# The last taps of the second depthwise convolution ahead of the key and value blocks of an encoder layer

## The chip, the cores and the metric

The kernel runs on one core of a Trainium2 chip. The metric is device time in microseconds (us) of one execution. Several executions of the kernel before gave a median of 944.46 us (the lowest 943.23). One more execution was profiled: it took 943.95 us, of which the profile covers a span of 941.9 us, from the first to the last instruction. What the profile calls PE is TensorE's matmul, PEld its weight load, DVE is VectorE, ACT is ScalarE, POOL is GpSimd and SP is SyncE, which here issues all DMAs.

## The reference

One layer over two sequences (256 and 2048 tokens of width 1024, with 16 meta tokens ahead of each):

```
h = rmsnorm(z, norm_w)
proj = einsum('bld,de->ble', h, w_in)
q, k, v, g_att, c_val, c_glu, g_conv = split(proj)
q = rmsnorm(q per head); k = rmsnorm(k per head)
att = windowed_gqa(q, k, v, sink) * silu(g_att)
u = c_val * sigmoid(c_glu)
y = depthwise_conv(u, conv_w, width 31) + conv_b
cnv = silu(layernorm(y, ln_w, ln_b)) * silu(g_conv)
out = z + einsum('ble,ed->bld', concat[att, cnv], w_out)
```

The convolution has 512 channels; the LayerNorm is over these channels, for each token.

## The kernel before, in words

The tokens are 18 blocks of 128 (numbers 0 to 17) and 16 meta columns, in six groups of three blocks, and the groups are two chunks: chunk 0 holds groups 0 to 2, chunk 1 groups 3 to 5 (blocks 9 to 17). The combined projection has eleven units of 256 columns. For each chunk they run in the order `ORDER`: four convolution units (`U_C`, 0 to 3), two gates of the convolution (`U_GC`, 4 and 5), two gates of the attention (`U_GA`, 9 and 10), then keys and values (`U_KV`, 8), then two units of queries (`U_Q`, 6 and 7). Each float32 product is made of three passes over split operands (`PASSES`), so one 128 by 256 block of `proj_te` (L873 to L887) is 24 matmuls at L879, and `proj_et` (L856 to L871) is 24 matmuls of up to 400 columns at L863.

After the projections comes the attention of 18 blocks with the output projection (L609). Its first steps are woven into the query units by `spread` (L658): at its 4th query block `attention_open` (L255) issues the first attention loads, at the 7th `q_prep(0)` runs, from the 8th on slots of the attention are handed out, and at the 9th `mixing_open` (L280) takes the memory of the convolution.

A chunk's convolution is four strips of 31 taps, each tap one DVE instruction over 128 by 1167 elements (L946; the first tap is L937), which adds to the strip `y`. The strips of odd and of even units wait in two lists, `conv_q`.

**What sets the order.** The program is written out in the order in which Python hands instructions out, and a scheduler may then move an instruction within its engine's order, by its own estimate of when operands are ready; the engines run that fixed order. Python's order around the projections is set by a ledger. After each block a `tick(ns)` (L177) adds the block's estimated nanoseconds to `credit`; while the credit is positive it takes taps from `conv_q`, at 1.04 * 1167 + 135 = 1348.7 each, and what is left over is dropped. Other DVE work is charged with `owe` (800 for one key and value block). A gate's half is worth 3912, a key and value or a query block 2640. `later(k, f)` hands `f` out at the end of the k-th tick from here; `store` is a DMA from SP two ticks on.

**Keys and values.** `kv_block` (L1023): 24 matmuls into one of four PSUM banks (tags a and b, two each); ACT makes two squared sums (L985) and the copy `vs` (L1028), POOL the inverse root `rqk` (L148, L149), DVE the low part of `vs` (L1029) and the scaled keys `kn` (L1037); PE transposes `kn` (L1047, tag d), ACT and DVE make `ks` (L1049, L1050); SP stores `vd` and, twice, `kd`.

**LayerNorm.** `ln_block` (L211) works on one block of 128 tokens: four transposes on PE (`lnt`, L221, tag c), statistics on DVE (L224, L225), an inverse root and an offset on POOL (L148, L149, L227), the normalised `zn` on DVE (L234; three buffers), four transposes back (`lnu`, L240, tag d or, once the attention is open, a), four Silu on ACT (L243), and a store `cd` by SP (L246). The last gate unit of a chunk puts its LayerNorm blocks into `ln_q` (L1247): blocks 0 to 7 for chunk 0, 8 to 17 for chunk 1. `tick` hands out at most one of them, when `ready` (L1241) says so: the chunk's last tap has been handed out, this was first seen at tick `seen`, and `LN_WAIT[c]` more ticks have passed.

Ahead of the last two units of the second chunk stands a loop that empties the lists of taps (`keys[-2]` is the first unit of queries of chunk 1):

```
1194  if (c, u) == keys[-2] and g == CHUNKS[c][0]:
1195      while conv_q[0] or conv_q[1]:
1196          tick(3000)
```

In the ledger of the kernel before, chunk 1 comes to its first key and value block (block 9) with a credit of -992 and seven taps left, all of the last strip. The ticks of blocks 9 to 13 hand out 1, 1, 2, 1 and 2 of them. The tick of block 14 finds none left; with `LN_WAIT[1]` = 1 the tick of block 15 hands out the first LayerNorm block, and those of blocks 16 and 17 and of the first seven query blocks the other nine. The loop finds the lists empty and does nothing.

Of the kernel before, what the change touches and what calls it, by code (L numbers as in the profile page):

```python
# [45 lines left out]
CACHE = 2  # L46
WST = 9
W0 = 3
LN_WAIT = (9, 1)
LTAGS = "dbdbd" + "dcdcddddd"  # L50
LTAGS_N = len(LTAGS)
MAN1 = {mybir.EngineType.Pool}
# [33 lines left out]
CHUNKS = [[0, 1, 2], [3, 4, 5]]  # L86
# [3 lines left out]
U_KV = 8  # L90
# [9 lines left out]
def hymba_kernel(  # L100
# [61 lines left out]
    def later(k, f):  # L162
        due.setdefault(clock[0] + k, []).append(f)
# [13 lines left out]
    def tick(ns):  # L177
        credit[0] += LOAD * ns
        if ln_q and not flushing[0] and ln_q[0][0]():
            ln_q.pop(0)[1]()  # L180
            ln_at[0] = clock[0]
            credit[0] -= 800
        while credit[0] > 0 and (conv_q[0] or conv_q[1]):
            side[0] ^= 1
            q = conv_q[side[0]] or conv_q[1 - side[0]]
            cost, f = q.pop(0)
            credit[0] -= cost
            f()
        credit[0] = min(credit[0], 0.0)
        clock[0] += 1  # L190
        for f in due.pop(clock[0], []):
            f()
# [508 lines left out]
    if True:  # L701
# [31 lines left out]
        class Prep:  # L733
# [6 lines left out]
            def load(self, d2):  # L740
                n = self.n
                self.xt[d2] = sp.tile([P, 2, 400], F32, tag="xt", name=f"xt{self.g}_{d2}", bufs=XTB)
                nc.sync.dma_start(
                    self.xt[d2][:, :, :n],
                    zt[2 * d2 : 2 * d2 + 2, :, self.c0 : self.c0 + n].rearrange("d p n -> p d n"),
                )
# [147 lines left out]
        def u_tiles(c, j):  # L894
            us[c, j] = cp.tile([P, UWID], F32, tag="us", name=f"us{c}_{j}")
            if c == 0:
                nc.gpsimd.memset(us[c, j][:, 271:286], 0.0)
            else:
                nc.gpsimd.tensor_copy(us[c, j][:, 0:30], carry[:, j, :])
                nc.gpsimd.memset(us[c, j][:, 1182:1197], 0.0)  # L900

        def c_group(c, j, ws, g):
            n = GROUPS[g][1]
            pg = proj_et(ws, 0, g)
            sg = sp.tile([P, 400], F32, tag="sg", name=f"sg{c}_{j}_{g}")
            nc.scalar.activation(sg[:, :n], pg[:, :n], AF.Sigmoid)  # L906
            tick(24 * (n / 2.4 + 3))
            pv = proj_et(ws, 1, g)
            if g == 0:
                dst = [(us[c, j][:, 0:271], 1, 272), (us[c, j][:, 286:301], 1, 16), (us[c, j][:, 301:429], 272, 400)]  # L910
            elif c == 0:
                o = 301 + 384 * g - 256
                dst = [(us[c, j][:, o : o + n], 0, n)]
            else:
                o = 30 + 384 * (g - 3)
                dst = [(us[c, j][:, o : o + n], 0, n)]
            for ap, a, b in dst:
                nc.vector.tensor_tensor(ap, pv[:, a:b], sg[:, a:b], op=ALU.mult)
            owe(600)
            tick(24 * (n / 2.4 + 3))  # L920
# [45 lines left out]
        def g_group(ws, t0, g):  # L966
            o = NM if g == 0 else 0
            for hi in range(2):
                ps = proj_et(ws, hi, g, o)
                so = gp.tile([P, 384], F32, tag="go", name=f"go{t0}_{hi}_{g}")  # L970
                nc.scalar.activation(so, ps[:, :384], AF.Silu)  # L971
                store(gd[t0 + hi, :, 384 * g : 384 * g + 384], so)
                tick(24 * 163)
# [86 lines left out]
        def kv_group(ws, g):  # L1060
            if g == 0:
                kv_block(ws, 0, 0, NM, -1)
                tick(24 * 107)
            for b in range(3 * g, 3 * g + 3):
                kv_block(ws, g, blk_local(b)[1], P, b)
                tick(24 * 110)

        ORDER = U_C + U_GC + U_GA + [U_KV] + U_Q
        keys = [(c, u) for c in range(2) for u in ORDER]
# [82 lines left out]
        def at_item_start(i, c, u, g):  # L1152
            if (c, u, g) == (1, ORDER[0], CHUNKS[1][1]):
                nc.sync.dma_start(km.bitcast(F32), kmd)
                for r0 in range(0, P, NM):
                    nc.sync.dma_start(vm[r0 : r0 + NM].rearrange("p a e -> p (a e)").bitcast(F32), vmd)
            if i == 0:
                for q in range(4):
                    w01[1][1](q, nc.gpsimd if q % 2 else nc.vector)
                for k in (4, 5, 6):  # L1160
                    r[k]()
            if i == 1:
                later(1, preps[1].first)
                later(1, preps[1].alloc)
                later(1, lambda: preps[1].scale(0))
                for q in range(4):
                    if q < 3:
                        later(1, lambda q=q: preps[1].scale(q + 1))
                    later(1, lambda q=q: preps[1].split(q))
                for k in range(7, 10):  # L1170
                    later(1, lambda k=k: later(1, stats(k)))
                for q in range(4):
                    later(2, lambda q=q: preps[2].load(q))
            if i == I2:
                later(1, preps[2].first)
                later(1, preps[2].alloc)
                later(1, lambda: preps[2].scale(0))
                for q in range(4):
                    if q < 3:
                        later(1, lambda q=q: preps[2].scale(q + 1))  # L1180
                    later(1, lambda q=q: preps[2].split(q))
# [9 lines left out]
        split_at += [(1, u, CHUNKS[1][1]) for u in U_C[1:]]  # L1191

        for i, (c, u, g) in enumerate(items):
            if (c, u) == keys[-2] and g == CHUNKS[c][0]:
                while conv_q[0] or conv_q[1]:
                    tick(3000)
            if u in U_C and g == CHUNKS[c][0]:
                u_tiles(c, u)
            ws = wsplit[c, u]
            at_item_start(i, c, u, g)  # L1200
            for t, p, what in prep_at.get(i, []):
                if what == "load":
                    for q in range(4):
                        later(1, lambda p=p, q=q: p.load(q))
                else:
                    later(1, p.first)
                    for q in range(4):
                        later(1 + q // 2, lambda p=p, q=q: p.scale(q))
            if u in U_C:
                c_group(c, u, ws, g)  # L1210
            elif u in U_Q:
                q_group(ws, u - U_Q[0], g, spread if (c, u) in keys[-2:] else lambda b: None)
            elif u == U_KV:
                kv_group(ws, g)
            elif u in U_GC:
                g_group(ws, 4 + 2 * (u - U_GC[0]), g)
            else:
                g_group(ws, 2 * (u - U_GA[0]), g)
            for k in loads.get(i, []):
                load, split = weights(k)  # L1220
                load(nc.sync)
                room = max(1, when[first_at[keys[k]]] - when[i + 1])
                for q in range(4):
                    at = max(1, min(room, W0 + q * min(WST, max(1, (room - 2) // 4))))
                    later(at, lambda split=split, q=q: split(q, nc.vector))
            if (c, u, g) in split_at:
                presplit_wo(split_at.index((c, u, g)))
            if c == 0 and u in U_GA:
                for k3 in range(3):
                    k = 10 + 3 * (3 * (u - U_GA[0]) + g) + k3  # L1230
                    if k <= NB:
                        later(1 + k3, lambda k=k: later(1, stats(k)))
            if (c, u) == (0, ORDER[-1]):
                p = preps[g + 3]
                p.alloc()
                for q in range(4):
                    later(1 + q // 2, lambda p=p, q=q: p.split(q))
            if u in U_C and g == CHUNKS[c][2]:
                conv(c, u, 0)
            if i == last_at[c, u] and u == U_GC[-1]:  # L1240
                def ready(c=c):  # L1241
                    if left[c, 0]:
                        return False
                    seen.setdefault(c, clock[0])
                    return clock[0] >= seen[c] + LN_WAIT[c]

                for b in range(0, 8) if c == 0 else range(8, NB):  # L1247
                    ln_block(c, b, ready)
# [66 lines left out]
```

## Time and profile before

| | |
|---|---|
| median of the runs | 944.46 us |
| profiled execution | 943.95 us |
| its span | 941.9 us |
| PE busy | 935.6 us (99%) |
| PEld busy | 886.3 us (94%) |
| DVE busy | 744.4 us (79%) |
| ACT busy | 421.8 us (45%) |
| POOL busy | 293.3 us (31%) |
| DMA | 176.49 MB, 187 GB/s on the mean |

The share of busy time is a mean over stages. A matmul's record is longer than the time until the next one starts, since matmuls are pipelined, so a busy PE shows only waits that are longer than that overlap; PEld, whose records are shorter, shows more of them. "Idle before" names what ended an engine's idle time. A row of the windows gives, for a stretch of the span, the busy time of each engine with the count of its instructions in brackets.

### The profile page before, as it was taken

The page shows a single profiled execution, that of the slowest core. Times are in us where ns is not written, and L with a number is a line of the kernel's source. Part 1 is how long each engine was busy: PE and PEld are TensorE (multiplying, and loading weights), DVE is VectorE, ACT ScalarE, POOL GpSimd, SP SyncE. Part 2 cuts the span into 40 slices and gives each one's busy share as a digit, 9 for nine tenths or more (in the row PEclk, how much of TensorE's full clock was granted, in tenths as well). Part 3 has the DMA queues.
Part 4 walks back from the last instruction along what each step waited for, and adds up shares of the span by engine and source line. Part 5 has one row for each costly group of instructions (what it writes and reads, how often), then busy time and mean ns, then how long its engine had stood idle before and what let it go on. Part 6 is the DMA issues. An engine that isn't in the chain of part 4 may idle for free.

```text
span 941.9 us, 16665 instructions
## 1 busy us (share of the span) xinstructions
PE 935.6 (99%) x5794; PEld 886.3 (94%) x5794; DVE 744.4 (79%) x1263; ACT 421.8 (45%) x1160; POOL 293.3 (31%) x490
## 2 busy tenths in 40 slices
PE   9999999999999999999999999999999999999998
PEld 8999999999999999999999999988888888888887
DVE  5579999997977879999996655677777677767773
ACT  7432022253457751011111356666666666656661
POOL 4320000173558400000000553755433242333332
PEclk9999999999999999999999999999999999999999
DMA  8575345676656595233333697975666556655512
GB/s 306 170 253 217 134 176 176 217 269 251 182 185 189 182 312 182 90 113 134 140 128 123 159 327 225 395 240 159 200 188 172 151 165 196 188 159 148 163 62 68
DMA packets 146211, 176.49 MB, mean 187 GB/s; under 512 B 40816, under 2 KB 108736, under 8 KB 146000
## 3 DMA queue, kind: packets, MB, share of 16 engines
q1 hardware_dynamic: 146128, 175.43, 57.8%
q8 instruction: 46, 0.75, 0.3%
q14 instruction: 37, 0.30, 0.1%
HBM read 112.69 MB, written 62.70 MB: 186 GB/s over the span
## 4 chain that ended last, share of the span: by engine, by line
PE 94%; DMA 2%; DVE 1%; SPq 1%; issue 0%; ACT 0%; POOL 0%; DVEq 0%; ACTq 0%; POOLq 0%
PE pj L863 43%; PE y L609 21%; PE pj L879 13%; PE O L533 5%; PE S L383 4%; PE pT_c L499 2%; PE pT_m L499 2%; PE pT_x L499 1%; DMA cd<-zn 1%; DMA bias<-in_bias_c 1%; PE qT L383 1%; PE lnu L240 0%; DMA xn<-in_z 0%; PE lnt L221 0%; DVE xt L772 0%
## 5 line engine op out<-in xcount | busy, mean ns | idle before, releaser
L863 PE MATMUL pj<-xh,ws 128*128 128x384 f32 (+1 forms) x1536 | 395.9, 338 | 0.1
L946 DVE SCALAR_TENSOR_TENSOR y<-us,cw,y 128x1167 f32<-128x1167 f32 x240 | 329.0, 1427 | 0.4
L863 PEld LDWEIGHTS pj<-xh,ws 128*128 128x128 f32 x1536 | 280.0, 188 | 0.4 <-ACT xh L1111 0.4
L863 PE MATMUL pj<-xl,ws 128*128 128x384 f32 (+1 forms) x768 | 260.9, 340 | 0.1
L609 PE MATMUL y<-wo,rest 128*128 128x512 f32 (+1 forms) x672 | 172.7, 394 | 0.0
L879 PE MATMUL pj<-ws,xh 128*128 128x256 f32 (+1 forms) x880 | 164.2, 284 | 0.3 <-DVE kn L1037 0.3
L863 PEld LDWEIGHTS pj<-xl,ws 128*128 128x128 f32 x768 | 144.1, 188 | 0.5 <-DVE xl L801 0.4
L609 PEld LDWEIGHTS y<-wo,rest 128*128 128x128 f32 x672 | 117.5, 189 | 21.4 <-DVE rest L566 0.3
L879 PEld LDWEIGHTS pj<-ws,xh 128*128 128x128 f32 (+1 forms) x880 | 136.1, 187 | 1.1 <-issue 0.4
L879 PE MATMUL pj<-ws,xl 128*128 128x256 f32 (+1 forms) x440 | 124.3, 283 | 0.0
L441 DVE CUSTOM_DVE_ANT_0 sb<-S,bias,vec 128x304 f32<-128x304 f32 (+5 forms) x144 | 74.5, 517 | 33.8 <-PE S L383 31.5
L453 ACT ACTIVATE sb<-sb,nm 128x304 f32<-128x304 f32 (+5 forms) x144 | 77.8, 540 | 48.9 <-DVE nm L441 48.2
L971 ACT ACTIVATE go<-pj 128x384 f32<-128x384 f32 x48 | 23.5, 489 | 149.8 <-PE pj L863 142.3
L879 PEld LDWEIGHTS pj<-ws,xl 128*128 128x128 f32 (+1 forms) x440 | 82.2, 187 | 0.2
L479 POOL TENSOR_SCALAR sb<-sb,es 128x304 f32<-128x304 f32 (+5 forms) x144 | 73.1, 525 | 16.0 <-DVE es L466 13.1
L561 POOL TENSOR_TENSOR at<-at,ga 128x256 f32<-128x256 f32 x36 | 26.5, 737 | 164.0 <-DVE at L555 104.8
L148 POOL TENSOR_SCALAR ssk<-ssk 128x2 f32<-128x2 f32 x18 | 8.4, 465 | 210.0 <-ACT sqk L985 210.0
L383 PEld LDWEIGHTS S<-kw,q 128*128 128x128 f32 x288 | 53.2, 188 | 10.6
L383 PE MATMUL S<-kw,q 128*128 128x304 f32 (+5 forms) x288 | 62.8, 299 | 0.0
L148 POOL TENSOR_SCALAR ssq<-ssq 128x4 f32<-128x4 f32 (+2 forms) x55 | 23.5, 427 | 98.3 <-ACT xn L726 74.4
L906 ACT ACTIVATE sg<-pj 128x384 f32<-128x384 f32 (+1 forms) x24 | 11.8, 492 | 82.9 <-PE pj L863 82.0
L609 PE MATMUL y<-wo,mch 128*128 128x512 f32 x144 | 47.2, 409 | 0.0
(139 smaller groups left out, 1306.9 us busy)
## 6 DMA issues: line engine op xcount, KB each, us to landing
wd<-ws SPq DMA_DIRECT2D x36, 512.0 KB, 5.8
ws<-wd SPq DMA_DIRECT2D x36, 512.0 KB, 6.2
wraw<-in_w_in SPq DMA_DIRECT2D x52, 256.0 KB, 6.3
xn<-in_z SPq DMA_DIRECT2D x18, 512.0 KB, 5.5
gd<-go SPq DMA_DIRECT2D x48, 192.0 KB, 2.2
yo<-in_z SPq DMA_DIRECT2D x36, 256.0 KB, 3.9
out_y<-yo SPq DMA_DIRECT2D x35, 256.0 KB, 2.7
wo<-wod SPq DMA_DIRECT2D x16, 512.0 KB, 7.4
```

The costliest lines, as they stand in the source:

```text
L148: nc.gpsimd.tensor_scalar(src, src, scale, eps, op0=ALU.mult, op1=ALU.add)
L383: r = f(*a, **k)
L441: nc.vector.tensor_tensor_reduce(out=sb[:, n, c0:c1], in0=ps[:, 0:w], in1=cst["bias"][:, kv, at + c0 : at + c1], scale=1.0, scalar=nsnk[:, ...
L453: nc.scalar.activation(sb[:, n, c0:c1], sb[:, n, c0:c1], AF.Exp, bias=nm[:, n : n + 1], scale=-1.0, accum_out=rs[:, n : n + 1],)
L479: nc.gpsimd.tensor_scalar(sb[:, k, a0:a1], sb[:, k, a0:a1], es[:, k : k + 1], 1.0, op0=ALU.mult, op1=ALU.mult)
L499: nc.tensor.transpose(pt[: c1 - c0, n, :], sbt[b, kv][:, n, c0:c1], ident)
L533: nc.tensor.matmul(opj[b, kv][:, n0:n1], t[:r, kv, :], p[:r, n0:n1], start=(k == "c" and i == 0), stop=(k == "x" and i == len(work) - 1),)
L561: nc.gpsimd.tensor_tensor(at[:, pr, :], at[:, pr, :], gat[b][:, pr, :], op=ALU.mult)
L609: nc.tensor.matmul(ps, mh[mi][:, e % 4, :], wo[e, wi][:, cols], start=(e == 4 and k == 0), stop=(e == 3 and k == 2),)
L863: nc.tensor.matmul(ps[:, :n], ws[:, d, wi, P * half_i : P * half_i + P], x[xi][:, d, o : o + n], start=(k == 0), stop=(k == 3 * ND - 1),)
L879: nc.tensor.matmul(ps[:rows, :UW], x[xi][:, d, o : o + rows], ws[:, d, wi, :], start=(k == 0), stop=(k == 3 * ND - 1),)
L946: nc.vector.scalar_tensor_tensor(y[:, yo + o0 : yo + o1], u[:, o0 + k : o1 + k], cw[:, j, k : k + 1], y[:, yo + o0 : yo + o1], op0=ALU.mul ...
```

## The change

The loop that empties the lists of taps runs ahead of the first key and value block of chunk 1, three items (nine blocks) earlier, and LayerNorm of chunk 1 waits two ticks in place of one after the lists have been seen empty.

```diff
-LN_WAIT = (9, 1)
+LN_WAIT = (9, 2)
...
         for i, (c, u, g) in enumerate(items):
-            if (c, u) == keys[-2] and g == CHUNKS[c][0]:
+            if (c, u) == (1, U_KV) and g == CHUNKS[c][0]:
                 while conv_q[0] or conv_q[1]:
                     tick(3000)
```

## The prediction

> **What bounds the kernel now.** I read the page first, for the busy shares and the chain that ended last.
>
> ```profile
> PE 935.6 (99%) x5794; PEld 886.3 (94%) x5794; DVE 744.4 (79%) x1263; ACT 421.8 (45%) x1160; POOL 293.3 (31%) x490
> ...
> PE 94%; DMA 2%; DVE 1%; SPq 1%; issue 0%; ACT 0%; POOL 0%; DVEq 0%; ACTq 0%; POOLq 0%
> ```
>
> PE is the bound, and nothing in this change takes work from PE or adds any: the taps are DVE work, and the LayerNorm blocks keep their eight transposes each. The change can only gain what PE waits for in the stretch that it reorders, and can only lose through new PE waits. So the second view was the waits, of PE and of PEld, over the whole span.
>
> ```profile
> PE warmup L1096 <- POOL ident masks.py:199: 1.4, 1, 1.4
> PE lnu L240 <- DVE zn L234: 0.7, 1, 0.7
> PE xt L1103 <- DVE xn L1131: 0.5, 2, 0.4
> PE pj L879 <- DVE kn L1037: 0.3, 1, 0.3
> ```
>
> ```profile
> PEld lnu L240 <- ACT qr L1004: 0.8, 1, 0.8
> PEld lnu L240 <- DVE zn L234: 0.3, 1, 0.3
> ```
>
> Columns are us in total, times, longest. One wait belongs to the second chunk's LayerNorm: `lnu`, the transpose back, waits for `zn`. PE shows 0.7 us of it, PEld 0.8 + 0.3 = 1.1. The third view was the windows around the stage.
>
> ```profile
> core 0: us, PE busy (x) PEld busy (x) DVE busy (x) ACT busy (x) POOL busy (x), PEclk, DMA share, GB/s
> ...
> 511.00:607.00 96.00, 95.30 (x803) 94.39 (x802) 55.29 (x148) 49.81 (x169) 47.28 (x102) 1.00 0.84 271
> 577.00:607.00 30.00, 30.00 (x248) 29.48 (x247) 18.82 (x62) 19.38 (x60) 16.86 (x36) 1.00 0.96 345
> ...
> 505.70:514.70 9.00, 9.00 (x63) 9.00 (x62) 0.00 (x0) 1.75 (x7) 0.06 (x1) 1.00 0.38 134
> ```
>
> From the first key and value block (511) to the end of the projections (607) PE idles 96.00 - 95.30 = 0.70 us, PEld 1.61 us. That is the whole purse. The clock is full.
>
> **The change part by part.** First the taps. By the ledger the second chunk reaches block 9 with credit -992 and seven taps. The moved loop gives 3000 a turn: 2008 buys two taps (at 1348.7) and leaves -690, then 2310 buys two, 2613 two, 2915 the last: four turns, all seven taps ahead of block 9 in program order. The DVE timeline shows where they ran before.
>
> ```profile
> 497.40 8.28 DVE L946 SCALAR_TENSOR_TENSOR y<-us,cw,y 128x1167 f32<-128x1167 f32 x6
> 514.75 0.29 DVE L1029 TENSOR_TENSOR vs<-pj,vs 128x128 fp32r<-128x128 f32 x1 [9.07 <-ACT vs L1028]
> 514.96 1.43 DVE L946 SCALAR_TENSOR_TENSOR y<-us,cw,y 128x1167 f32<-128x1167 f32 x1
> ...
> 522.75 1.42 DVE L946 SCALAR_TENSOR_TENSOR y<-us,cw,y 128x1167 f32<-128x1167 f32 x1
> ```
>
> ```profile
> 511.00:607.00 96.00, 7.12 (x5) 1.00 0.84 271
> ```
>
> Five taps (the window of that line alone: five, 7.12 us) run after `vs` of block 9; so two of the seven were already ahead of it. DVE stood idle for 9.07 us until 514.75. Run back to back a tap takes 8.28 / 6 = 1.38 us, so the five end at 505.68 + 5 x 1.38 = 512.6, and `vs` of block 9 starts at 514.75 as now. **The taps cost nothing**, hidden in that idle time. If the cover were gone (the five starting only when block 9 starts, 510.8), they would end at 517.7 and block 9's `vs` be 3 us late; block 13 is the first that needs its PSUM bank, four blocks of 2.84 us, 11.4 us, after block 9 began. Bounds: 0 to 0.
>
> Second, LayerNorm's place. Block 9's tick now sees the empty lists, and two ticks on, after block 11, the first LayerNorm block is handed out; the others follow blocks 12 to 17 and the first three query blocks. Before, the first followed block 15. That is four blocks earlier, though the wait is a tick longer.
>
> ```profile
> 510.96 8.17 PE pj L879 x69
> ...
> 529.83 0.11 PE kt L1047
> ...
> 534.75 0.44 PE lnt L221 x4
> ...
> 537.43 0.45 PE lnu L240 x4
> ```
>
> ```profile
> 531.20 0.60 PE L221 MATMUL lnt<-ident,y 128*128 128x128 f32 x4
> ...
> 575.22 0.63 PE L240 MATMUL lnu<-ident,zn 128*128 128x128 f32 x4 [0.66 <-DVE zn L234]
> ```
>
> A matmul of 256 columns costs 8.17 / 69 = 0.118 us, a block 24 x 0.118 = 2.84. The first `lnt` moves from 531.2 to about 510.8 + 3 x 2.84 = 519.4, long after the last tap (512.6), so no wait on `y` arises. The last `lnu` moves from 575.2 to after the 13th block: 510.8 + 13 x 2.84 + 9 x 0.11 + 10 x (0.44 + 0.45) = 557.6. Work for PE: the same instructions, 0.
>
> Third, the wait that goes. `zn` of the last LayerNorm block started at 574.27, when a store of an earlier `zn` had landed, and `lnu` could only follow it:
>
> ```profile
> 574.27 0.81 DVE L234 TENSOR_SCALAR zn<-lnt,mv 128x512 f32<-128x512 f32 x1 [4.00 <-DMA cd<-zn]
> ```
>
> ```profile
> 552.29 0.70 SPq L269 DMA_DIRECT2D bias<-in_bias_c  x1
> ...
> 563.34 0.54 SPq L303 DMA_DIRECT2D kw<-kd  x1
> ...
> 570.72 1.75 SPq L246 DMA_DIRECT2D cd<-zn  x1
> ```
>
> That store was late because SP's queue is in order and the attention's first loads, handed out after the fourth query block, stood ahead of it (552 to 570). With the last LayerNorm block handed out after the third query block, most of the stores are issued before those loads, and three buffers of `zn` suffice. So the lnu wait goes: between 0.7 us (PE's row) and 1.6 us (PEld's idle time in the stretch). I take **1.0 us**, near PEld's own row for that wait (1.1).
>
> [...]
>
> What is late next? The first attention step. It was at 578.41, and a 1.5 MB load goes ahead of its DVE step:
>
> ```profile
> 578.41 0.36 PE L383 MATMUL S<-kw,q 128*128 128x176 f32 x2
> ```
>
> ```profile
> bias<-in_bias_c SPq DMA_DIRECT2D x1, 1520.0 KB, 9.5
> ...
> cd<-zn SPq DMA_DIRECT2D x10, 256.0 KB, 3.3
> ```
>
> Issued at 552.3, it landed at 561.8, 16 us early. LayerNorm work of about 3 us moves from behind the opening to ahead of it, so the loads may be issued 3 us later, and the first S comes 1 us earlier: 12 us of cover remain. From 577 on PE is full (30.00 of 30.00), so a gain there is kept to the end. SP is also moved past: the four turns of the loop advance the clock by four ticks, so the last gate stores are handed out before, not between, the key and value blocks; they wait for ACT as before and nothing on PE waits for them. Cost 0.
>
> Fourth, seven instead of three LayerNorm blocks now fall among key and value blocks. Mean ns of one, from the groups of the stretch:
>
> ```profile
> L243 ACT ACTIVATE zn<-lnu,vec 128x128 f32<-128x128 f32 x40 | 15.0, 457 | 10.0 <-PE lnu L240 9.9
> ...
> L149 POOL TENSOR_TENSOR rqk<-ssk,half 128x2 f32<-128x2 f32 x9 | 8.7, 962 | 0.7
> L234 DVE TENSOR_SCALAR zn<-lnt,mv 128x512 f32<-128x512 f32 x10 | 8.1, 805 | 10.7 <-DMA cd<-zn 8.4 <-POOL mv L227 2.3
> ...
> L224 DVE BATCH_NORM_STATS2 bs<-lnt 128x6 f32<-128x512 f32 x10 | 7.0, 695 | 2.5 <-PE lnt L221 2.4
> ...
> L149 POOL TENSOR_TENSOR mv<-mv,half 128x1 f32<-128x1 f32 x10 | 5.5, 550 | 0.6
> ...
> L985 ACT ACTIVATE sqk<-pj 128x64 f32<-128x64 f32 x18 | 4.1, 225 | 9.1 <-PE pj L879 6.8 <-POOL rqk L149 2.0
> L985 ACT ACTIVATION_READ_ACCUMULATOR sqk<-pj 128x1 f32 x18 | 3.6, 200 | 0.0
> L1049 ACT ACTIVATE ks<-kt,kscale 128x128 fp32r<-128x128 f32 x9 | 3.3, 369 | 7.0 <-PE kt L1047 3.6 <-DMA kd<-ks 3.3
> L1050 DVE SCALAR_TENSOR_TENSOR ks<-kt,kscale,ks 128x128 fp32r<-128x128 f32 x9 | 3.1, 347 | 1.7 <-ACT ks L1049 1.6
> ```
>
> One period on PE is 2.84 + 0.11 + 0.44 + 0.45 = 3.84 us. ACT has in it 15.0 / 10 = 1.5 for four Silu, 2 x (0.225 + 0.200) + 0.369, and a copy of `vs` that I estimate at 0.3 (like DVE's 0.29): 3.0. DVE has 0.805 + 0.695 + 0.347, 0.29 each for `vs` and `kn` (estimated alike), and an aggregation I estimate at no more than 0.3: 2.7. POOL has at most 0.96 + 0.55 and three small steps, about 2.3 by estimate. All fit under 3.84, and the two blocks after 531.2 that already run this mix show no PE wait (the only lnu waits are the rows above). Value 0; the bound above is seven waits of the longest kind seen, 7 x 0.8 = 5.6.
>
> **Sum** against the profiled execution: 943.95 - 0 - 1.0 + 0 = 942.95, say 942.9. That execution lies between the undisturbed runs (943.23 and 944.46), 0.5 under the median shown.
>
> **Rivals.** *Nothing comes of it*: the lnu wait goes, but a later instruction of PE that was just in time (a transpose or matmul of the query stage whose operand comes from ACT) waits as long. For: 1 us is less than half a block, and ACT has waits on both sides of it. Against: from 577 on PE is full. Time: 943.95 (943.2 to 944.5 with the runs' spread).
>
> *Slower*: the `cd` stores now share SP's in-order queue with the `vd` and `kd` stores of the key and value blocks, each of which holds the queue until its operand is ready:
>
> ```profile
> SPq L195 <- DVE vs L1029: 6.7, 4, 2.7
> ```
>
> `zn` then waits for its buffer, and `lnu` for `zn`, at each of the seven blocks. The price is 0.8 us each: 943.95 + 5.6 = 949.6. It decides once a store comes more than two periods, 7.7 us, after its Silu; landing takes 3.3 and the longest wait of `zn` now is 4.0, so I think it unlikely.
>
> *All of PEld's idle time goes*: 943.95 - 1.6 = 942.3. For: the PEld row; against: 0.5 of it has other releasers.
>
> *The change doesn't do what it says*: the scheduler already put two of seven taps ahead of `vs`, and could place the first `lnt` late again if its own estimate has the taps end late. Then the lnu wait stays: 943.95, counted with the first rival.
>
> **How the numbers follow.** Forecast 0.60, nothing 0.25, all of PEld's idle time 0.05, slower 0.08, something no row shows 0.02. Range: from 942.3 less the runs' spread (943.95 - 943.23 = 0.7), 941.6, to the first rival's upper end, 944.5, with one new wait of 0.8: 945.3. It leaves out most of the slower case. A change over 2% (18.9 us), about what a measurement of this kernel can tell from none, is reached by no case; I keep 0.01 for faster and 0.02 for slower, since a new wait can repeat and the purse is small.
>
> **What would show it.** In the changed profile: seven or more taps in a row ahead of the first `vs`, with no idle time of about 9 us between; no tap of L946 after about 514; first `lnt` near 519 (not 531), last `lnu` near 558; no PE or PEld row of lnu waiting for `zn`; the DVE row of `zn` waiting for `cd` gone or far under 8.4 us; PE 95.9 or more of 96 in the stretch. Wrong would be: rows of PE waiting for `kn`, `zn` or a PSUM bank between 511 and 560, a first S that waits for a load, or a span that moves by more than 3 us either way.

## The result, and the profile after

The changed kernel took a median of 947.24 us (946.92 to 950.93, six runs) against 943.58 us for the kernel before on the same chip: ratio 1.0046, interval [1.0028, 1.0064]. One of the six executions of the kernel before took 1543.74 us, and the ratio leaves it out. The forecast was 942.9 us in a range of 941.6 to 945.3. The change costs some 4 us where I had it win 1. The profiled execution took 950.93 us with a span of 949.1: it is the longest of the six; a second profile of the same kernel (`e1_again`, below) is nearer to it.

The page first, then PE's waits (us in total, times, longest).

```profile
PE 939.1 (99%) x5794; PEld 889.7 (94%) x5794; DVE 744.9 (78%) x1263; ACT 421.5 (44%) x1160; POOL 294.8 (31%) x490
```

```profile
PE pj L879 <- ACT sqq L980: 3.5, 1, 3.5
...
PE pj L879 <- PE lnu L240: 0.8, 1, 0.8
PE O L533 <- ACT ptiles L515: 0.5, 1, 0.5
...
PE lnu L240 <- DVE zn L234: 0.2, 1, 0.2
```

The instructions are as many as before. The wait of `lnu` for `zn` shrank from 0.7 to 0.2 us, as meant. Three new ones stand above it. The largest, 3.5 us (3.7 by PEld), lies in the query units (`pj` is the PSUM tile of a projection, `sqq` the squared sum that ACT makes of it), and the change doesn't touch these units. The windows show where:

```profile
511.00:607.00 96.00, 91.79 (x773) 90.71 (x771) 51.47 (x135) 43.81 (x153) 46.70 (x101) 1.00 0.79 251
577.00:607.00 30.00, 26.86 (x224) 26.25 (x222) 15.34 (x49) 14.48 (x46) 16.12 (x35) 1.00 0.93 309
...
607.00:613.00 6.00, 5.19 (x29) 5.11 (x30) 3.66 (x10) 4.41 (x14) 0.00 (x0) 0.72 0.98 368
```

PE was full in 577 to 607 before (30.00 of 30.00); now 26.86. Its idle time in 511 to 607 rose from 0.70 to 4.21 us, another 0.81 us lies after 607, and there the granted clock fell to 0.72. The chain of work that ended last shows what PE waited for (start, us, what), and the timelines of ACT and of SP's queue (SPq) name the rows:

```profile
590.26 3.71 DMA qd<-qr
...
594.05 0.37 ACT qr L1004
...
599.86 7.21 DMA qd<-qr
...
607.10 0.28 ACT qr L1004
607.38 0.38 ACT sqq L980
...
607.81 4.55 PE pj L879 x24
```

```profile
607.10 0.37 ACT L1004 COPY qr<-pj 128x256 f32<-128x256 f32 x1 [5.92 <-DMA qd<-qr]
```

```profile
561.89 0.45 SPq L329 DMA_DIRECT2D q<-qd  x1
...
564.37 0.65 SPq L269 DMA_DIRECT2D bias<-in_bias_c  x1
...
596.30 3.46 SPq L329 DMA_DIRECT2D q<-qd  x1
599.86 1.45 SPq L195 DMA_DIRECT2D qd<-qr  x3
```

Read from the end: PE's block of queries at 607.81 needs a PSUM bank that ACT frees; ACT, in its fixed order, stood for 5.92 us at the copy `qr` (L1004), whose buffer was still being stored; that store was issued at 599.86, behind a load that had held SP for 3.46 us, and took 7.21 us to land. Over all stores `qd<-qr` the median from issue to landing rose:

```profile
qd<-qr SPq DMA_DIRECT2D x14, 128.0 KB, 2.3
```

```profile
qd<-qr SPq DMA_DIRECT2D x14, 128.0 KB, 3.8
```

The first row is of before, the second of after. The 24 matmuls that follow the wait took 4.55 us, 190 ns each, against 118 ns: another 1.7 us. Together (4.21 + 0.81 - 0.70) + 1.7 = 6.0 of the 7.2 us by which the span grew; some 0.8 more lies ahead of the whole stretch (the first `kt` of a block stands at 234.4 against 233.6, in code that the change leaves alone).

What had begun late is the attention's first load: the bias load was issued at 564.37, against 552.29 before, 12 us later. It stands behind the last store of keys in SP's order:

```profile
559.97 1.24 SPq L195 DMA_DIRECT2D kd<-ks  x2
```

```profile
544.87 1.77 SPq L195 DMA_DIRECT2D kd<-ks  x2
```

The first row is of after, the second of before. The keys are late because `kt` (L1046) and `lnu` (L238) share the two PSUM banks of tag d, in the order in which the program hands them out. Once LayerNorm blocks are handed out between key blocks, a `kt` takes the bank of an `lnu`, and that `lnu` has the whole chain of its block ahead of it. PE's timeline after:

```profile
525.15 0.27 PE L1047 MATMUL kt<-ident,kn 128*128 128x128 f32 x1
...
533.53 0.60 PE L240 MATMUL lnu<-ident,zn 128*128 128x128 f32 x4
...
534.40 0.27 PE L1047 MATMUL kt<-ident,kn 128*128 128x128 f32 x1
```

Before, the same two `kt` ran at 524.38 and 526.85.

And the taps? They did not move. DVE's timeline and the window of that line alone:

```profile
515.55 0.29 DVE L1029 TENSOR_TENSOR vs<-pj,vs 128x128 fp32r<-128x128 f32 x1 [10.38 <-ACT vs L1028]
515.76 1.42 DVE L946 SCALAR_TENSOR_TENSOR y<-us,cw,y 128x1167 f32<-128x1167 f32 x1
...
523.55 1.42 DVE L946 SCALAR_TENSOR_TENSOR y<-us,cw,y 128x1167 f32<-128x1167 f32 x1
```

```profile
511.00:607.00 96.00, 7.12 (x5) 1.00 0.79 251
```

Five taps still follow `vs` of block 9, with the idle time of some 10 us still ahead of them: the loop changed the order in which the taps are handed out, and the scheduler put them back. So the last tap ends at 524.97, and the first LayerNorm blocks, handed out earlier, wait for it:

```profile
520.24 0.49 PE L221 MATMUL lnt<-ident,y 128*128 128x128 f32 x3
...
526.68 0.38 PE L221 MATMUL lnt<-ident,y 128*128 128x128 f32 x2
```

Three transposes of the first block run at 520.24; the fourth, which reads the last strip, comes after the last tap, at 526.68, and the block's `lnu` only at 533.53.

### The profile page after: what moved, and what is told of

It is laid out like the page before. It is cut to its first block, busy times and chain, and to the rows that moved or that the text cites. A ratio compares the mean times of both kernels' runs of the same rounds, so it can differ in the third digit from the quotient of the medians.

```text
span 949.1 us, 16661 instructions
## 1 busy us (share of the span) xinstructions
PE 939.1 (99%) x5794; PEld 889.7 (94%) x5794; DVE 744.9 (78%) x1263; ACT 421.5 (44%) x1160; POOL 294.8 (31%) x490
## 4 chain that ended last, share of the span: by engine, by line
PE 93%; DMA 3%; DVE 1%; issue 1%; ACT 1%; SPq 1%; POOL 0%; DVEq 0%; ACTq 0%
PE pj L863 42%; PE y L609 21%; PE pj L879 14%; PE O L533 5%; PE S L383 4%; PE pT_c L499 2%; PE pT_m L499 2%; PE pT_x L499 1%; DMA qd<-qr 1%; DMA cd<-zn 1%; PE qT L383 1%; DMA wraw<-in_w_in 1%; PE lnt L221 1%; PE lnu L240 1%; DMA gc<-gd 1%
## 5 line engine op out<-in xcount | busy, mean ns | idle before, releaser
L148 POOL TENSOR_SCALAR ssq<-ssq 128x4 f32<-128x4 f32 (+2 forms) x55 | 26.5, 481 | 105.5 <-ACT xn L726 70.6
```

The costliest lines, as they stand in the source:

```text
L148: nc.gpsimd.tensor_scalar(src, src, scale, eps, op0=ALU.mult, op1=ALU.add)
```

## The experiments

My first theory: **late keys**. LayerNorm among the key blocks holds the banks of tag d, so the keys are late, so the attention's loads are late, and these collide with the query stores. Rivals: the taps' place itself; the sharing of banks on PE's side; a smaller pool of buffers than needed, whatever is late.

**e1_again**, the changed kernel once more.

> The changed kernel unaltered, as the control of this set and for a second profile of it. All theories: about 947.2 us (946.9 to 948), slower than the kernel before by 3 to 4.5 us. K-chain theory: the last store of kd near 560 us and the load of bias near 564 us again (545 and 552 in the kernel before), and one wait of PE of 2 to 4 us in the query units, for ACT, between 590 and 610 us. If the slow clock after that wait (0.72 in the stretch 607 to 613 of the first profile) is a consequence of it, it shows here again only if the wait is as long.

947.63 us (946.24 to 949.18), ratio 1.0035 [1.0023, 1.0048]. Its waits:

```profile
PE pj L879 <- ACT sqq L980: 1.6, 2, 1.2
PE pj L879 <- issue: 1.1, 1, 1.1
PE O L533 <- ACT ptiles L515: 0.8, 1, 0.8
```

The loss repeats, the single wait of 2 to 4 us does not: in the same order of instructions the loss comes out in several smaller waits, two of them for `sqq` of at most 1.2 us. The bias load stands at 564.01.

**e2_loop_alone**, the loop moved, LayerNorm at its old place.

```
-LN_WAIT = (9, 2)
+LN_WAIT = (9, 6)
```

> The moved loop alone: LN_WAIT[1] is 6 instead of 2, so that LayerNorm of the second chunk is handed out after block 15 as in the kernel before. K-chain theory: the taps stand where they stood on DVE, so 943.6 us, within 0.5 us of the kernel before, bias load near 552 us. Taps theory (it is the seven taps handed out ahead that cost): about 947 us as with the whole change.

943.58 us, ratio 0.9993 [0.9985, 1.0002]; the bias load at 552.63. The loop alone does nothing: PE, DVE, ACT and POOL then run the same instructions in the same order as in the kernel before. The taps theory falls; all of the effect is LayerNorm's place.

The profiled execution of e2 (942.86 us, span 940.8) shows one thing more. It ran the order of the kernel before, and `lnu` did not wait at PE:

```profile
511.00:607.00 96.00, 96.00 (x809) 95.22 (x808) 56.43 (x150) 50.37 (x171) 48.48 (x105) 1.00 0.83 276
```

From 10 to 567 us PE's instructions start within 0.1 us of those in the profile of before. At the two `lnu` that before ran at 567.64 and 575.22, e2 gains 0.3 and 0.7 us, and that lead of 1.04 us is still there at the end of the span.

**e3_own_bank**, the changed kernel with chunk 1's `lnu` in tag c.

```
-tag="d" if phase[0] == 1 else "a"
+tag=("c" if c else "d") if phase[0] == 1 else "a"
```

> The changed kernel, but the transposes back of LayerNorm (lnu) of the second chunk take their PSUM banks from tag c instead of d, so that the transposes of the keys (kt) share d with nothing. K-chain theory: kt runs once per block again, the last store of kd comes near 545 us instead of 560, the load of bias near 552, and the wait of PE in the query units is gone: 942.5 to 944.5 us. Stores theory (the cd stores of LayerNorm among the key and value blocks, or LayerNorm's work on DVE and ACT there, are what costs, whatever the banks): still 946.5 to 948.

952.41 us, ratio 1.0082 [1.0068, 1.0096]: slower yet. The mechanism holds by half: the keys are on time again (last store at 545.96, bias load at 552.28) and the wait for `sqq` is gone. But `lnu` now shares tag c with `lnt` and the attention's O, LayerNorm is late in its turn (last `cd` store at 591.91), and another wait has its place:

```profile
PE pT_m L499 <- DVE q L406: 3.6, 1, 3.6
```

I had looked at the bank that was freed and not at the one that was taken.

**e4_late_keys**, the kernel before with only the keys late.

```
-                later(1, fin2)
+                later(4 if b >= 9 else 1, fin2)
```

(and five buffers of `kn`, so that nothing else holds).

> The kernel before, with its LayerNorm where it was, but the transpose of the keys of each block of the second chunk is handed out three ticks later (and kn has five buffers so that nothing waits for it). K-chain theory: late keys alone do the harm; the last store of kd comes 8 to 15 us later than 545 us, the load of bias with it, and the time is 945.5 to 948 us, with PE waiting for ACT in the query units. Stores theory: late keys do not matter, 943 to 944.5 us.

947.34 us, ratio 1.0033 [1.002, 1.0045], with LayerNorm and taps about as in the kernel before (first `lnt` at 531.69 against 531.20). Waits and loads:

```profile
PE pj L879 <- ACT sqq L980: 2.0, 1, 2.0
PE pj L879 <- DVE ks L1050: 0.9, 1, 0.9
```

```profile
559.59 1.24 SPq L195 DMA_DIRECT2D kd<-ks  x2
...
563.31 0.61 SPq L269 DMA_DIRECT2D bias<-in_bias_c  x1
```

Late keys alone bring about the same loss, with a wait for `sqq` as in the changed kernel. That is the strongest support for the theory. The row for `ks` is a cost of late keys without any load: a query block waits for a bank of tag d that a late `kt` holds.

**e5_wait4** and **e6_wait3**, LayerNorm two blocks and one block later than in the changed kernel (`LN_WAIT = (9, 4)` and `(9, 3)`).

> The changed kernel with LN_WAIT[1] = 4: LayerNorm of the second chunk is handed out after block 13, two blocks earlier than in the kernel before and two later than with the change. In the program's order the nine transposes of the keys (kt) then stand one per block again. K-chain theory: last store of kd at 548 us or before, bias load at 556 or before, no wait of PE for ACT in the query units: 943 to 944.7 us, though LayerNorm is earlier. Stores theory (the earlier LayerNorm starts, the more it costs): half way, 945.3 to 946 us.

> The changed kernel with LN_WAIT[1] = 3: LayerNorm is handed out after block 12. In the program's order the last four transposes of the keys stand one block later than in the kernel before (three later with the change). K-chain theory: last store of kd 3 to 6 us later than 545 us, little or no wait of PE in the query units: 943.6 to 945.5 us. Stores theory: 946 to 947 us.

Both missed: 947.13 us, ratio 1.0039 [1.0026, 1.0053], and 949.55 us, ratio 1.006 [1.0048, 1.0073]. The loads came earlier, to 556.11 and 559.41, and the wait for `sqq` went; but a wait of the kind that the change was to remove is there instead, 1.7 us in e5 and 3.0 in e6. In e5:

```profile
PE lnu L240 <- DVE zn L234: 1.7, 1, 1.7
```

```profile
566.43 0.81 DVE L234 TENSOR_SCALAR zn<-lnt,mv 128x512 f32<-128x512 f32 x1 [7.35 <-DMA cd<-zn]
```

```profile
556.11 1.87 SPq L269 DMA_DIRECT2D bias<-in_bias_c  x1
...
561.72 0.80 SPq L246 DMA_DIRECT2D cd<-zn  x1
```

DVE waited 7.35 us for one of `zn`'s three buffers, whose store came behind the bias load and other loads in SP's order. So the theory needed a second part: the late traffic reaches PE through whichever buffer it drains next.

**e7_four_buffers**, the changed kernel with four buffers of `go`, `qs` and `qr` in place of three.

> The changed kernel with four instead of three buffers for the query copies (qr, qs) and the gates (go). It tests the last link: PE waits in the query units because ACT, which works in order, waits for a buffer of qr, whose store by SP is late. K-chain theory: loads and key stores as late as with the change (bias near 564 us), but the wait of PE for ACT sqq is gone or under 0.5 us: 944.8 to 946.2 us; the wait of pj for lnu near 560 us stays. If it were the late loads themselves that PE waits for, it would stay at 947 to 948 us.

946.12 us, ratio 1.0028 [1.0016, 1.0039]. As expected: the wait for `sqq` is gone, the bias load is still at 564.34; `pj` waits 1.0 us for a bank of tag d, and O 1.0 us for `ptiles`. That the wait goes is shown; that the time falls is not clear, since the interval overlaps that of e1.

**e8_first_bank**, the changed kernel with the first query block after the opening in a bank of tag a instead of d (`LTAGS` begins with "a").

> The changed kernel, but the first query block after the opening of the attention takes its PSUM bank from tag a instead of d (LTAGS begins with a). Bank theory: the wait of 1.2 us near 560 us, in which that block's first matmul waits until ACT has read the last lnu out of its bank of d, is gone, and nothing else changes: 946.0 to 946.8 us, 1 us under the changed kernel. If that wait is only passed on to the query units, 947 to 948 us.

947.77 us, ratio 1.005 [1.0037, 1.0064]: that wait is gone, and 0.8 us at `lnu`, 1.5 us at O and 0.7 us at `pj` stand in its place. Passed on, not won.

The next runs ask whether the buffers carry the loss.

**e9_wait4_zn5**, e5 with five buffers of `zn`.

```
-st["zn"] = yp.tile([P, 512], F32, tag="zn", name=f"zn{b}", bufs=3)
+st["zn"] = yp.tile([P, 512], F32, tag="zn", name=f"zn{b}", bufs=5)
```

> The second value of LN_WAIT is 4 and zn has five buffers in place of three. If the wait of 1.7 us of lnu for zn, with LayerNorm started two blocks later than in the changed kernel, came from zn's three buffers (the DVE write of zn waiting 7.35 us for the store into cd, which stood behind attention loads in SP's order), that wait falls under 0.5 us, the first query unit still doesn't wait, and the time comes to 943.5 to 945.5 us. Rival: the 3 us are the price of kt and lnu taking turns in two PSUM banks, or of the order of PE's work, whatever the stores do; then it stays at 946 to 948 us.

943.57 us, ratio 1.0003 [0.9994, 1.0012]: the 3 us of e5 are back, with `kt` and `lnu` taking turns in tag d as in e5. The scheduler re-places some instructions of this stretch when a buffer count changes, so the two kernels differ in a little more than the buffers.

```profile
511.00:607.00 96.00, 95.60 (x805) 94.64 (x804) 56.65 (x149) 50.34 (x171) 47.57 (x103) 1.00 0.84 270
```

The bias load is at 556.26. In this kernel loads that are 4 us late cost nothing: PE is busy for 95.60 of 96 us.

**e10_before_covers**, the kernel before with five of `zn` and four of `go`, `qs`, `qr`.

> The kernel before with five buffers of zn and four of go, qs and qr. This asks what there was to win. In the trace of before PE's matmuls lose 1.1 us in 550 to 575 and 0.2 us in 575 to 607 beyond their own durations, so no order of LayerNorm could give back more than some 1.3 us: 942.5 to 944.2 us, ratio 0.9985 to 1.000. Rival: the waits of this stretch cost more than those 1.3 us because they delay the stage behind it; then it is below 942 us.

943.59 us, ratio 1.0004 [0.9995, 1.0012]. The `lnu` wait of before is gone, and the median is not lower. The order of PE changes with these buffers too, and another wait stands late in the query units, as it does in e9:

```profile
PE O L533 <- DVE ptiles L516: 0.4, 1, 0.4
```

So e10 shows that this kernel wins nothing. It does not show that the wait for `zn` was worth nothing: the pair of profiles under e2 has it at 1.0 us.

**e11_after_covers** and, for a second profile, **f5_after_covers_again**: the changed kernel with the same buffers.

> The changed kernel with five buffers of zn and four of go, qs and qr. The keys and the attention loads stay late (last store of keys near 559.6, bias load near 564), but both buffers through which the late stores reach PE are deeper. If the loss reaches PE through those buffers, neither the wait for sqq nor that of lnu for zn is left, and only the wait for a bank of tag d at 560 (1.0 us) and that of O for ptiles (0.5 to 1.0) remain: 944.5 to 946 us. Rival: the late loads cost PE their time by another road (attention begins later, or wo and cn arrive later); then it stays at 946.5 to 948 us.

> The changed kernel with five buffers of zn and four of go, qs and qr, once more. By e11 a median of 945.5 to 947.5 us. If the rest comes from PE's waits for O's ptiles behind late loads, the trace shows 1 to 3 us of them in 575 to 613; if the rest lies elsewhere (a lower granted clock without a new wait), the waits stay at 1.2 us and the clock column of the windows falls below 1.00.

946.92 us (944.58 to 948.12), ratio 1.0036 [1.0022, 1.005], and 946.12 us (944.42 to 949.51), ratio 1.0024 [1.0011, 1.0036]. Its fastest executions reach 944.5, its median does not. The bias load stays at 563.6 in both profiles, and in f5 ACT waited 3.70 us for a store even with four buffers, so that O waited at PE, and the granted clock fell behind it:

```profile
605.94 0.37 ACT L1004 COPY qr<-pj 128x256 f32<-128x256 f32 x1 [3.70 <-DMA qd<-qr]
```

```profile
PE O L533 <- ACT ptiles L515: 2.5, 1, 2.5
```

```profile
607.00:613.00 6.00, 5.64 (x20) 4.47 (x21) 3.22 (x10) 3.38 (x11) 4.06 (x11) 0.72 1.01 363
```

The expectation of e11 missed; its rival, a road of its own for late loads, holds in part. That of f5 held: the median lies in its range, and 2.7 us of waits for `ptiles` lie between 575 and 613.

**f3_after_zn5** and **f4_wait3_zn5**: five buffers of `zn` alone, in the changed kernel and in e6.

> The changed kernel with five buffers of zn alone. In the changed kernel lnu waited only 0.2 us for zn, so by the theory (there it is the query buffers that carry the lateness to PE) little is recovered: the bias load stays after 563, the wait for sqq of 1 to 3.5 us stays, 945.8 to 947.8 us. Rival: zn's buffers are what matters at every LN_WAIT; then 943.5 to 944.8 us.

> The second value of LN_WAIT is 3 and zn has five buffers. With three buffers it took 949.55 us with a wait of 3.0 us of lnu for zn. By the theory that wait goes and the bias load stays near 559: 943.5 to 945.5 us. Rival: 946 us or more, with another wait in its place.

947.27 us, ratio 1.0028 [1.0017, 1.0039], as the theory had it, though in that profile, the fastest of its eight executions, the wait sat at O (2.4 us) and not at `sqq`, right behind a wait of ACT of 3.62 us for a store of `qd`; and 946.26 us, ratio 1.0016 [1.0007, 1.0024]: the 3.0 us at `lnu` went, but O and `pj` wait 1.7 us in their place, so the expectation missed and its rival holds, though more than half of e6's loss is gone. With `zn` out of the way, time follows the lateness of the loads; but these four kernels differ in the place of LayerNorm as well, and the table can't tell the two apart:

| kernel | `LN_WAIT[1]` | last `kd` store | bias load | median | ratio to before |
|---|---|---|---|---|---|
| e10_before_covers | 1, loop behind | 544.98 | 552.16 | 943.59 | 1.0004 |
| e9_wait4_zn5 | 4 | 552.02 | 556.26 | 943.57 | 1.0003 |
| f4_wait3_zn5 | 3 | 553.46 | 558.88 | 946.26 | 1.0016 |
| f3_after_zn5 | 2 | 558.09 | 563.66 | 947.27 | 1.0028 |

(e10 has four buffers of `qr` as well.)

**f6_late_keys_covers**, e4 with the buffers of e10.

> The kernel before with the transposes of the keys of blocks 9 and on three blocks later (as e4) and five buffers of zn, four of go, qs and qr. LayerNorm is as in before. Late keys alone took 947.34 us. If the late stores reach PE through those buffers, the wait for sqq goes and the time falls to 943.5 to 945.5 us. If late keys cost by a road of their own as well, it stays at 946 to 948 us, like e11.

947.09 us (944.45 to 950.38), ratio 1.003 [1.0016, 1.0044]. Late keys cost by a road of their own as well: in its profile, the slowest of its ten executions, no store holds ACT, but the output projection waits for its weights, `wo`, which stand behind all of this in SP's order. Its chain and waits:

```profile
605.96 8.06 DMA wo<-wod
614.02 0.04 issue
614.07 0.73 PE y L609 x2
```

```profile
PE y L609 <- DMA wo<-wod: 2.8, 2, 1.8
PE pj L879 <- DVE ks L1050: 1.1, 1, 1.1
```

**e12_wait8**, LayerNorm two blocks later than in the kernel before.

> The second value of LN_WAIT is 8: LayerNorm begins two blocks later than in the kernel before. The keys have tag d to themselves up to the last blocks, so the last store of keys stays before 546 and the bias load before 554; the first query unit doesn't wait. The last stores of cd come some 7 us later than in before, among the attention loads, so by the theory of the stores one wait of lnu for zn of 0.7 to 2 us may show: 943.3 to 945.5 us. Rival: the earlier LayerNorm starts, the dearer it is, without regard to what stands in SP's queue; then a later start costs nothing or gains, 942.5 to 943.8 us, with no new wait.

953.57 us (951.66 to 955.41), ratio 1.0105 [1.0091, 1.0119]. Both expectations missed. The bias load is on time (551.74), but LayerNorm now runs on into the attention's first steps: its POOL, DVE and ACT steps stand in the chain between theirs, PE is busy for 4.34 of 7 us in 600 to 607, and the clock falls to 0.74 in 607 to 613. The old place lies between two slopes, keys late on one side and attention steps late on the other.

**f1_loads_2_later** and **f2_loads_3_later** were to make the loads alone late, in the kernel before (`if n == 4` in `spread` becomes 6 and 7).

> The kernel before with the attention stage opened at the sixth query block in place of the fourth; keys, LayerNorm and tag d are as in before. The bias load moves from 552 to some 558 us. If late loads by themselves are the harm, part of the loss shows: 944.5 to 946.5 us, with a wait of PE between 560 and 610 that before doesn't have. If lateness up to that point still lies within the cover (as the load at 556 of e9 did), 943.3 to 944.5 us.

> The kernel before with the attention stage opened at the seventh query block, the block at which the first queries are prepared; keys, LayerNorm and tag d are as in before. The bias load moves to some 561 to 564 us, as late as in the changed kernel (564). If late loads by themselves are the harm: 946 to 949 us, with a wait of a query unit for sqq, or of lnu for zn, of over 1 us. Rival (keys and LayerNorm in the two banks of tag d, or PE's order, are the harm): 943.3 to 944.8 us.

954.16 us, ratio 1.0096 [1.0082, 1.011], and 953.64 us, ratio 1.0094 [1.008, 1.0108]. Neither is a test: the bias load stayed at 553.68 and 552.71, since the scheduler put the loads back, while the order of PE, ACT and DVE changed in many places. What f1 shows is the road through `zn` once more: `lnu` waited 5.2 us for it in one piece. Lateness of the loads with everything else as before could not be had this way, and stays untested by itself.

## Why the prediction was wrong

**The taps cost nothing: right in the sum, wrong in the step.** "All seven taps ahead of block 9 in program order" holds in the ledger, but the scheduler orders DVE by its own estimate, and five still ran after `vs` of block 9. The last tap ends at 524.97, not 512.6. e2 measures the loop by itself at 0, within its interval.

**LayerNorm's place: about right for its start, late for its end.** The first `lnt` was foreseen at 519.4 and starts at 520.24; but "no wait on `y` arises" failed with the taps, and the last `lnu` came at 565.09 instead of 557.6.

**The wait that goes: right in place and in size, and not seen in any median.** PE's row fell from 0.7 to 0.2 us. For the execution that was profiled, 1.0 us was the right price, and "a gain there is kept to the end" held: the profile of e2, in the same order without this wait, is 1.04 us shorter, nearer to PEld's rows for that wait (1.1) than to PE's (0.7), and the whole lead is made at the two `lnu`. But that is one execution against another of the same order, so the same order can run with the wait and without it. e9 and e10, without the row, run in the time of the kernel before, with a wait of 0.4 us at O; this is what my first rival said, though that the one became the other is not shown. The rival in which all of PEld's idle time goes, a gain of 1.6, did not come: in e2, without a wait of PE in the stretch, 0.78 us of PEld's idle time stays there (95.22 of 96).

**What is late next: the step that failed.** I let the loads be "issued 3 us later", and left "12 us of cover". They came 12 us later. The bias load took 9.0 us to land, at 573.4, and the first step that reads it ran at 579.50, so some 6 us of cover were left, and the first attention step was hardly late (`S` at 579.10 against 578.41); but I had asked only about the first user of the loads. Behind them in the same order of SP stand the `cd` and `qd` stores and the `wo` loads, and DMA in 575 to 607 was at 0.96 already. In the kernels of the table above, with `zn` given room, 4 us late cost nothing (e9), 6.7 us late went with a loss of 0.16%, 1.5 us (f4), and 11.5 us late with 0.28%, 2.6 us (f3).

**Seven LayerNorm blocks among the key blocks: value 0 was the reason for it.** I compared the engines' loads with PE's period of 3.84 us and found that all fit, and they do: in 536 to 550 of the changed kernel PE is busy for all 14.00 us, and no other engine for more than 8.81. I didn't look at the PSUM banks: `kt` and `lnu` take turns in two, so a key block had to wait for a whole LayerNorm chain: after the `kt` at 525.15 the next came only at 534.40, behind the first `lnu`, and the later ones 4.3 to 4.9 us apart. By the last block the `kd` store had slid by 559.97 - 544.87 = 15 us. The bound of 5.6 us would have covered the loss, but by luck: it was made of seven waits of `lnu` for `zn`, and the loss is something else.

**The rival that was nearest** was the slower one: stores in SP's queue, `zn` without a buffer, `lnu` late. Its mechanism is real (e5, e6, f1), but in the changed kernel itself it is worth 0.2 us; there the same lateness comes out at the query stores. I had it at 0.08.

Shown by the runs: the loop does nothing (e2), the shared banks make the keys late (e3), and late keys, with the order of PE's work that goes with them, make the loss without LayerNorm's move (e4). Made likely: that `zn`'s buffers carry the loss in e5 (e9, where some of the order changed too). Argued, not shown: that the loads' lateness is enough by itself (f1 and f2 failed to test it). And no kernel here beats the one before by more than its interval.

## What to carry to other kernels

Before moving a chain earlier, list what it shares with its new neighbours besides engines: PSUM tags, buffers, and the in-order queue that drains them; engines that "all fit" say nothing about a bank that two chains take in turns. When something is late, ask for everything behind it in its queue, not for its first user alone. A stall of under 1 us in one profile is no promise of 1 us: the next execution of the same order may not have it (e2), and with the waiting buffer given more room another wait may stand there (e10).

## What the runs showed of the hardware that I had not expected

A wait of PE of 3.5 us cost more than itself here. After that wait, in the profile of the changed kernel, the granted clock was 0.50 for the next 3.2 us:

```profile
604.00:607.80 3.80, 0.33 (x4) 0.09 (x1) 0.83 (x2) 0.70 (x3) 1.92 (x4) 0.98 1.05 394
607.80:611.00 3.20, 3.19 (x15) 3.19 (x16) 2.89 (x9) 3.10 (x10) 0.00 (x0) 0.50 0.96 357
```

The clock was back at 0.99 in 611 to 614. The same follows a wait of 3.0 us in e6 (0.58 in the 3.2 us behind it), of 2.5 in f5 (0.75 for 7 us) and of 5.2 in f1 (0.50 for 6 us); behind 2.4 us in f3 and 2.0 in e4 the clock stayed at 1.00. In these runs it is not the longest single wait alone that decides: in f6 two waits of 1.0 and 1.8 us between 610 and 614 were followed by 0.65 in the next 4 us, and in e12, where no wait there is longer than 1.3 us but PE is busy for only 4.34 of 7 us in 600 to 607, it was 0.74 in 607 to 613.

So one wait of 3.5 us became 5 us. e11 and f5 show it in a pair: they are the same kernel in the same order, and PE's instructions start within 0.1 us of each other up to 605. Then the wait at O is 1.5 us longer in f5, the clock falls there and not in e11 (1.00 in 607 to 613), and from 612 to the end f5 is 3.0 us behind. The spread within f5 goes with the clock: its ten executions took 944.42 to 946.38 us where the mean clock was 1.0 and 947.64 to 949.51 where it was 0.998 or 0.996. In e1 it doesn't: 949.18 us at 1.0, 946.24 at 0.999.
